# A gated recurrence's 128 by 128 score matmuls become pairs of 64-column tiles

## The chip, the cores and the metric

The kernel runs on one core of one Trainium2 chip. The metric is the device time of one execution in microseconds, the median of three runs. In the traces PE is TensorE (its matmuls; PEld are its weight loads), DVE is VectorE, ACT is ScalarE, POOL is GpSimd and SP is SyncE.

## The reference, cut to what matters

An encoder trunk of two layers is applied to two sequences, of 512 and of 256 tokens, with shared weights in fp32. Each layer is half a SwiGLU feed-forward, a token mixer, and another half feed-forward. Layer 0 mixes with a bidirectional gated linear recurrence (HGRN2), layer 1 with windowed attention. The recurrence is the part that is changed:

```python
def gla_chunk_scan(q, k, v, logf):
    """S_t = diag(f_t) S_{t-1} + k_t v_t^T, o_t = S_t^T q_t."""
    ...
o_fwd = gla_chunk_scan(q, k_f, i, logf_f)
rev = lambda a: jnp.flip(a, axis=1)
o_bwd = rev(gla_chunk_scan(rev(q), rev(k_b), rev(i), rev(logf_b)))
o = (o_fwd + o_bwd).astype(F32)
```

There are eight heads with keys and values of 128. Within 128 tokens the result is a 128 by 128 matrix A of scores (a query against each key, times all forget gates between the two) applied to the values; between such blocks a state is carried.

## The kernel before, in words

All 768 tokens of both sequences lie side by side, in six blocks of 128 (four and two). Feed-forward and projections split each fp32 factor into two parts of the faster fp32r type and sum three products (`mm3`, lines 254 to 256).

For each head `hgrn_proj` computes queries, keys and gates, transposed, with the 128 key channels on partitions. Then `hgrn_scan` builds A without ever dividing by a product of gates, over seven levels. At level l tokens form groups of 2^l, and level l fills the entries of A whose query and key lie in neighbouring groups of one pair. Level 6 thus fills the two 64 by 64 corners off the diagonal of a block, and levels 0 to 5 lie inside the two 64 by 64 corners on it. One more product, of the plain queries and the summed keys, fills the diagonal itself.

A level runs so:

1. ACT copies the level's keys together into `kop` (line 689), one buffer that all levels use.
2. PE multiplies, for each of the six blocks, `kop` by the level's queries (`scan_scores`, line 664): 128 by 128 by 128, in plain fp32. In the trace one such matmul is two weight loads and two MATMUL records. The blocks of the first sequence go to one PSUM bank, those of the second to another (`ps` tiles, eight banks in turn).
3. DVE merges the result into A (`put`): a copy at level 0 (line 678), and a copy under a mask of the level's entries elsewhere (line 683), one for each sequence.
4. DVE multiplies the queries by the gates (line 706), the keys by theirs (line 710) and the gates among themselves (line 712) for the next level. The queries may be changed only when PE has read them.

After the levels, the blocks' states and outputs follow (lines 726 to 765). `weave` issues the next head's projection in pieces between the levels of this one; the order on each engine is then set by the tile framework's scheduler, which the program leaves to it, and each engine runs its own instructions strictly in that order. Weights are staged ahead by ACT (line 166) and DVE (line 167).

Of the kernel before, what the change touches and what calls it, by code (L numbers as in the profile page):

```python
# [16 lines left out]
P = 128  # L17
# [5 lines left out]
T = TA + TB  # L23
NBLK = T // P
EPS = 1e-6
HEADS = 8
LEVELS = 7
# [6 lines left out]
SEQS = ((0, TA), (TA, TB))  # L34
# [13 lines left out]
class Trunk:  # L48
# [608 lines left out]
    def halves(self, t, l, par, d):  # L657
        return t[:, d, :].rearrange("p (b g j) -> p b g j", g=2, j=1 << l)[:, :, par, :]

    def scan_scores(self, pss, lhs, rhs):  # L660
        nc = self.nc
        for b in range(NBLK):
            s, i = (0, b) if b < 4 else (1, b - 4)
            nc.tensor.matmul(pss[s][:, i * P : (i + 1) * P], lhs(b), rhs(b), start=True, stop=True)  # L664

    def hgrn_scan(self, hd, v):
        nc = self.nc
        h, qs, kd, f, q, k = (hd[n] for n in ("h", "qs", "kd", "f", "q", "k"))
        ka = self.big([P, 2, T])
        kop, A = ka[:, 0, :], ka[:, 1, :]  # L670
        totals = self.big([P, 2, T])
        blk = lambda t, b: t[:, b * P : (b + 1) * P]

        def put(level, pss):
            for s, (off, n) in enumerate(SEQS):
                dst = A[:, off : off + n]
                if level == 0:
                    nc.vector.tensor_copy(dst, pss[s])
                    continue
                nb = n // P  # L680
                m = self.masks[:, level, :].unsqueeze(1).to_broadcast([P, nb, P])
                r = lambda t: t.rearrange("p (b j) -> p b j", b=nb)
                nc.vector.copy_predicated(r(dst), m, r(pss[s]))

        tot, base = f, 0
        for l in range(LEVELS):
            c, J = T >> l, 1 << l
            kv = bass.AP(k.tensor, k.offset, [list(k.ap[0]), [2 * J, c // 2], [T + J, 2], [1, J]])
            nc.scalar.copy(kop.rearrange("p (b g j) -> p b g j", g=2, j=J), kv)

            def rhs(b):
                return bass.AP(
                    q.tensor, q.offset + b * P, [list(q.ap[0]), [2 * J, P // (2 * J)], [T + J, 2], [1, J]]
                )

            pss = [self.ps(n) for _, n in SEQS]
            self.scan_scores(pss, lambda b: blk(kop, b), rhs)
            put(l, pss)
            if l == 0:
                pss = [self.ps(n) for _, n in SEQS]  # L700
                self.scan_scores(pss, lambda b: blk(kd, b), lambda b: blk(qs, b))
                put(LEVELS, pss)
            part = [list(q.ap[0])]
            both = bass.AP(q.tensor, q.offset, part + [[T + J, 2], [2 * J, c // 2], [1, J]])
            t = bass.AP(tot.tensor, tot.offset + base + 1, [list(tot.ap[0]), [T - 1, 2], [2, c // 2], [0, J]])
            nc.vector.tensor_mul(both, both, t)
            for d in range(2):
                xv = self.halves(k, l, d, d)
                t = tot[:, 1 - d, base + 1 - d : base + c : 2].unsqueeze(2).to_broadcast([P, c // 2, J])
                nc.vector.tensor_mul(xv, xv, t)  # L710
            nbase = 0 if l == 0 else base + c
            nc.vector.tensor_mul(
                totals[:, :, nbase : nbase + c // 2], tot[:, :, base : base + c : 2], tot[:, :, base + 1 : base + c : 2]
            )
            tot, base = totals, nbase
            yield

        F, Bk = 1, 0
        order = ((0, 0), (0, 1), (0, 2), (0, 4), (1, 1), (1, 2), (1, 3), (1, 5))
        kT = self.big([P, 8, P])  # L720
        S = self.big([P, 8, P])
        for half in range(2):
            pt = self.ps()
            for i in range(4):
                d, b = order[half * 4 + i]
                nc.tensor.transpose(pt[:, i * P : (i + 1) * P], blk(k[:, d, :], b), self.ident)
            nc.scalar.copy(kT[:, half * 4 : half * 4 + 4, :], pt.rearrange("p (a b) -> p a b", a=4))
        vb = lambda b: v[b][:, h * P : (h + 1) * P]
        pds = []
        for half in range(2):  # L730
            pd = self.ps()
            for i in range(4):
                d, b = order[half * 4 + i]
                nc.tensor.matmul(pd[:, i * P : (i + 1) * P], kT[:, half * 4 + i, :], vb(b), start=True, stop=True)
            pds.append(pd)
        state = {}
        for d, steps in ((0, ((0, None), (1, 0), (2, 1), (4, None))), (1, ((3, None), (2, 3), (1, 2), (5, None)))):
            for b, prev in steps:
                i = order.index((d, b))
                ds = pds[d][:, (i % 4) * P : (i % 4 + 1) * P]  # L740
                if prev is None:
                    nc.scalar.copy(S[:, i, :], ds)
                else:
                    dec = totals[:, 1 - d, base + b : base + b + 1]
                    nc.vector.scalar_tensor_tensor(S[:, i, :], S[:, order.index((d, prev)), :], dec, ds, ALU.mult, ALU.add)
                state[(d, b)] = S[:, i, :]
        yield
        pos = [self.ps(n) for _, n in SEQS]
        for b in range(NBLK):
            s, i = (0, b) if b < 4 else (1, b - 4)  # L750
            o = pos[s][:, i * P : (i + 1) * P]
            terms = [(blk(A, b), vb(b))]
            if (0, b - 1) in state and b != 4:
                terms.append((blk(q[:, F, :], b), state[(0, b - 1)]))
            if (1, b + 1) in state and b != 3:
                terms.append((blk(q[:, Bk, :], b), state[(1, b + 1)]))
            for j, (l_, r_) in enumerate(terms):
                nc.tensor.matmul(o, l_, r_, start=(j == 0), stop=(j == len(terms) - 1))  # L758
        for s, (off, n) in enumerate(SEQS):
            nb = n // P  # L760
            sq = self.tmp(n)
            nc.scalar.square(sq, pos[s])
            for b in range(nb):
                nc.scalar.copy(vb(off // P + b), pos[s][:, b * P : (b + 1) * P])
            nc.vector.tensor_reduce(
                self.hss[:, h, off // P : off // P + nb], sq.rearrange("p (b j) -> p b j", b=nb), AX.X, ALU.add
            )
# [507 lines left out]
```

## Time and profile before

| | |
|---|---|
| runs | 2866.38, 2866.47, 2860.94 us; median 2866.38 |
| span of the profiled execution, from the first to the last instruction | 2863.4 us |
| the recurrence's scan, eight heads | about 585 to 960 us of the span |
| MATMUL records of line 664 | 768 (two for each of 384 matmuls) |
| merges of lines 678 and 683 | 16 and 112 |
| granted TensorE clock, mean | 0.997 |

The profiled execution is one of its own; its page gives its span and no time beside it. A group of instructions in the profile is named by its line, engine, operation and tile; "128x512" is partitions by elements. Matmuls are pipelined, so a record's duration is longer than the distance from its start to the next one's. The chain of waits counts that distance, and the durations of records overlap.

### The profile page before, as it was taken

Reading aid. Unit: us, or ns where it says so; the run is one execution under the profiler, and the core shown is the slowest. Engines: PE = TensorE matmul, PEld = TensorE weight load, DVE = VectorE, ACT = ScalarE, POOL = GpSimd, SP = SyncE. Lnnn points to the kernel's source line nnn. Section 1 sums busy time; section 2 is a strip of 40 time slices with the busy share of each in tenths; the row PEclk is TensorE's granted clock in tenths of the full one; section 3 lists DMA queues with packets and bytes.
Section 4 is the critical chain, followed back from the end, with each engine's and each line's share of the span. In section 5 each row is a group of like instructions: output and inputs, shape, how many; then the busy total and the mean of one; then the engine's idle time right before and its main releaser. Section 6 shows DMA issues by size and latency. Waiting matters only on the chain.

```text
span 2863.4 us, 40520 instructions
## 1 busy us (share of the span) xinstructions
PE 2800.4 (98%) x15225; PEld 2556.8 (89%) x15225; DVE 2198.4 (77%) x3846; ACT 1318.5 (46%) x2454; POOL 304.4 (11%) x306
## 2 busy tenths in 40 slices
PE   8999999999999999999999999999999899999998
PEld 8899998889899889988998998999887779988997
DVE  7788788477577658788878877887859978778877
ACT  7344443434344435444445543444457755434443
POOL 1111120000000001111110111111000001111110
PEclk9999999999999999999999999999999999999999
DMA  6555454311111233555444355445412113554443
GB/s 166 126 124 125 116 133 119 109 45 38 52 38 30 74 88 89 133 129 124 118 118 109 88 134 126 121 119 122 126 63 74 45 38 92 132 129 120 120 122 96
DMA packets 330101, 291.37 MB, mean 102 GB/s; under 512 B 11608, under 2 KB 257840, under 8 KB 329904
## 3 DMA queue, kind: packets, MB, share of 16 engines
q1 hardware_dynamic: 294064, 212.43, 25.2%
q0 software_dynamic: 31680, 62.93, 12.5%
q10 hardware_dynamic: 4160, 13.42, 1.3%
q8 instruction: 119, 1.95, 0.3%
q14 instruction: 78, 0.64, 0.1%
HBM read 216.39 MB, written 9.44 MB: 79 GB/s over the span
## 4 chain that ended last, share of the span: by engine, by line
PE 68%; DVE 21%; DMA 5%; issue 3%; ACT 3%; DVEq 0%; ACTq 0%; POOLq 0%; SPq 0%
PE ps L414 24%; PE ps L472 11%; PE ps L254 8%; PE ps L255 8%; PE ps L256 8%; DVE w L200 5%; DVE big L260 3%; PE ps L664 3%; DVE x L494 3%; DMA wr<-wr 3%; DMA wr<-in_ffn_w_dram 3%; DVE tA L347 1%; DVE wr L206 1%; PE ps L758 1%; PE ps L316 1%
## 5 line engine op out<-in xcount | busy, mean ns | idle before, releaser
L414 PE MATMUL ps<-big,w 128*128 128x384 f32 x6720 | 1174.0, 335 | 6.6 <-DVE tA L437 6.2
L414 PEld LDWEIGHTS ps<-big,w 128*128 128x128 f32 x6720 | 1166.0, 188 | 12.7 <-DVE tA L437 11.2
L199 ACT CAST w<-wr 128x512 fp32r<-128x512 f32 x600 | 415.9, 707 | 724.2 <-PE ps L414 317.0
L472 PE MATMUL ps<-w,big 128*128 128x512 f32 x2520 | 587.2, 392 | 17.3 <-DVE x L494 17.3
L472 PEld LDWEIGHTS ps<-w,big 128*128 128x128 f32 x2520 | 470.4, 188 | 129.2 <-DVE x L494 16.6
L200 DVE TENSOR_TENSOR w<-wr,w 128x512 fp32r<-128x512 f32 (+1 forms) x520 | 437.1, 851 | 95.8 <-ACT w L199 87.1
L494 DVE SCALAR_TENSOR_TENSOR x<-ps,x 128x512 f32<-128x512 f32 x468 | 305.9, 683 | 20.4 <-PE ps L472 10.2
L141 POOL DMA_DIRECT2D s<-wr x120 | 105.6, 880 | 1619.8 <-DMA wr<-in_ffn_w_dram 585.7
L254 PE MATMUL ps<-w,big 128*128 128x512 f32 x624 | 248.9, 399 | 0.2
L256 PE MATMUL ps<-w,big 128*128 128x512 f32 x624 | 244.9, 393 | 2.2 <-DVE big L323 1.3
L255 PE MATMUL ps<-w,big 128*128 128x512 f32 x624 | 244.2, 391 | 0.0
L259 ACT CAST big<-tA 128x384 fp32r<-128x384 f32 x296 | 147.9, 513 | 178.9 <-DVE tA L442 77.1
L254 PE MATMUL ps<-big,w 128*128 128x384 f32 (+2 forms) x640 | 220.8, 346 | 3.4 <-ACT big L259 2.0
L255 PE MATMUL ps<-big,w 128*128 128x384 f32 (+2 forms) x640 | 216.9, 339 | 0.7 <-DVE big L260 0.5
L256 PE MATMUL ps<-big,w 128*128 128x384 f32 (+2 forms) x640 | 215.7, 337 | 0.0
L167 DVE TENSOR_TENSOR w<-wr,w 128x1024 fp32r<-128x1024 f32 x92 | 111.4, 1221 | 81.0 <-ACT w L166 56.9
L260 DVE TENSOR_TENSOR big<-tA,big 128x384 fp32r<-128x384 f32 x296 | 167.4, 576 | 8.1 <-ACT big L259 4.9
L205 DVE TENSOR_TENSOR wr<-wr,wr 128x512 f32<-128x512 f32 (+1 forms) x100 | 79.4, 794 | 119.1 <-DMA wr<-wr 89.7
L141 POOL DMA_DIRECT2D wr<-wr x100 | 87.2, 872 | 687.6 <-DVE tA L343 321.4
L166 ACT CAST w<-wr 128x1024 fp32r<-128x1024 f32 x92 | 96.6, 1052 | 120.3 <-PE ps L255 99.4
L256 PEld LDWEIGHTS ps<-w,big 128*128 128x128 f32 x624 | 117.1, 188 | 28.2 <-DVE big L323 2.0
L254 PEld LDWEIGHTS ps<-w,big 128*128 128x128 f32 x624 | 117.4, 188 | 22.4 <-issue 0.6
(170 smaller groups left out, 3296.8 us busy)
## 6 DMA issues: line engine op xcount, KB each, us to landing
wr<-in_ffn_w_dram SPq DMA_DIRECT2D x264, 512.0 KB, 3.9
s<-in_ffn_w_dram SPq DMA_DIRECT2D x120, 256.0 KB, 3.0
s<-wr POOLq DMA_DIRECT2D x120, 256.0 KB, 4.0
wr<-wr POOLq DMA_DIRECT2D x80, 256.0 KB, 3.8
wr<-in_hg_w_in_dram SPq DMA_DIRECT2D x40, 512.0 KB, 3.7
wr<-wr POOLq DMA_DIRECT2D x20, 512.0 KB, 4.6
spill<-x ACTq DMA_DIRECT2D x12, 512.0 KB, 3.1
x<-spill ACTq DMA_DIRECT2D x12, 512.0 KB, 3.3
```

Source lines behind the costliest of these rows:

```text
L141: self.nc.gpsimd.dma_start(out, src, accum_op=ALU.add)
L167: self.nc.vector.tensor_sub(lo, raw, hi.bitcast(F32))
L199: nc.scalar.copy(h, src)
L200: (eng or nc.vector).tensor_sub(l, src, h.bitcast(F32))
L254: nc.tensor.matmul(out, a[0], b[0], start=first, stop=False)
L255: nc.tensor.matmul(out, a[0], b[1], start=False, stop=False)
L256: nc.tensor.matmul(out, a[1], b[0], start=False, stop=last)
L259: self.nc.scalar.copy(hi, src)
L260: self.nc.vector.tensor_sub(lo, src, hi.bitcast(F32))
L414: self.nc.tensor.matmul(ps, a[x], b[y], start=first and k == 0 and i == 0, stop=k == 3 and i == 2, skip_group_check=True,)
L472: nc.tensor.matmul(ps, a[x], w[y], start=name == chain and kp == 0 and q == 0, stop=kp == 1 and q == 2, skip_group_check=True,)
L494: self.nc.vector.scalar_tensor_tensor(x, ps, c, x, ALU.mult, ALU.add)
```

## The change

Each 128 by 128 score matmul becomes two, for the two halves of a block's keys (`par`). Each has 64 columns of `kop` as weights, and streams only the 64 queries that those keys can meet: at levels 0 to 5 and for the diagonal those of the same half, at level 6 those of the other half. The first half writes partitions 0 to 63 of the bank, the second 64 to 127; in the instructions they are tiles of 128 rows by 64 columns of the array, at column 0 and at column 64. The corners that a level doesn't need are not computed any more. A level's scores are then 384 columns for both sequences, in one bank. The merge goes by partition halves, each over all six blocks; level 6 becomes a plain copy, since its corners are needed whole.

```diff
-    def scan_scores(self, pss, lhs, rhs):
-        nc = self.nc
+    def scan_scores(self, lhs, rhs):
+        ps = self.ps(NBLK * 64)
         for b in range(NBLK):
-            s, i = (0, b) if b < 4 else (1, b - 4)
-            nc.tensor.matmul(pss[s][:, i * P : (i + 1) * P], lhs(b), rhs(b), start=True, stop=True)
+            for par in range(2):
+                rows = slice(par * 64, (par + 1) * 64)
+                self.nc.tensor.matmul(ps[rows, b * 64 : (b + 1) * 64], lhs(b)[:, rows], rhs(b, par), start=True, stop=True)
+        return ps
...
-        def put(level, pss):
-            for s, (off, n) in enumerate(SEQS):
-                dst = A[:, off : off + n]
-                if level == 0:
-                    nc.vector.tensor_copy(dst, pss[s])
+        def put(level, ps):
+            for par in range(2):
+                rows = slice(par * 64, (par + 1) * 64)
+                c = 1 - par if level == LEVELS - 1 else par
+                dst = A.rearrange("p (b c j) -> p b c j", c=2, j=64)[rows, :, c, :]
+                src = ps[rows, :].rearrange("p (b j) -> p b j", j=64)
+                if level in (0, LEVELS - 1):
+                    nc.vector.tensor_copy(dst, src)
                     continue
-                nb = n // P
-                m = self.masks[:, level, :].unsqueeze(1).to_broadcast([P, nb, P])
-                r = lambda t: t.rearrange("p (b j) -> p b j", b=nb)
-                nc.vector.copy_predicated(r(dst), m, r(pss[s]))
+                m = self.masks[rows, level, c * 64 : (c + 1) * 64].unsqueeze(1).to_broadcast([64, NBLK, 64])
+                nc.vector.copy_predicated(dst, m, src)
...
-            pss = [self.ps(n) for _, n in SEQS]
-            self.scan_scores(pss, lambda b: blk(kop, b), rhs)
-            put(l, pss)
+            put(l, self.scan_scores(lambda b: blk(kop, b), rhs))
```

The scheduler's order changes with it on DVE. Its order at level 0 of the first head before (ps_5154 and ps_5155 are the banks of level 0, ps_5164 and ps_5165 those of the diagonal, big_5151 holds A, big_4938 the queries, big_4939 the keys, big_5152 the gates):

```order
L678 COPY big_5151<-ps_5154 128x512
L678 COPY big_5151<-ps_5155 128x256
L706 TENSOR_TENSOR big_4938<-big_4938,big_4937 128x2x384
L683 COPY_PREDICATED big_5151<-big_4691,ps_5164 128x512
L683 COPY_PREDICATED big_5151<-big_4691,ps_5165 128x256
L710 TENSOR_TENSOR big_4939<-big_4939,big_5152 128x192x2 x2
```

and after, where ps_5154 and ps_5169 are the two banks, and lines 708 and 712 are 706 and 710 of before:

```order
L683 COPY big_5151<-ps_5154 64x6x64 x2
L686 COPY_PREDICATED big_5151<-big_4691,ps_5169 64x6x64 x2
L708 TENSOR_TENSOR big_4938<-big_4938,big_4937 128x2x384
L712 TENSOR_TENSOR big_4939<-big_4939,big_5152 128x192x2 x2
```

The queries are now scaled behind the merge of the diagonal, where they were scaled ahead of it. On the other levels merge, queries and keys keep their order, except that in the fifth of the seven levels the keys are scaled in two parts, with a weight split between them.

More of the change, by code (lines that the diff above doesn't have):

```diff
@@ L689, in hgrn_scan, with rhs @@
             nc.scalar.copy(kop.rearrange("p (b g j) -> p b g j", g=2, j=J), kv)
[L691 to L694, printed above, removed]
-            pss = [self.ps(n) for _, n in SEQS]
-            self.scan_scores(pss, lambda b: blk(kop, b), rhs)
-            put(l, pss)
+            def rhs(b, par):
+                part = list(q.ap[0])
+                if J == 64:
+                    return bass.AP(q.tensor, q.offset + b * P + (0 if par else T + J), [part, [1, J]])
+                at = q.offset + b * P + par * 64
+                return bass.AP(q.tensor, at, [part, [2 * J, 64 // (2 * J)], [T + J, 2], [1, J]])
+            put(l, self.scan_scores(lambda b: blk(kop, b), rhs))
             if l == 0:
-                pss = [self.ps(n) for _, n in SEQS]
-                self.scan_scores(pss, lambda b: blk(kd, b), lambda b: blk(qs, b))
-                put(LEVELS, pss)
+                own = lambda b, par: qs[:, b * P + par * 64 : b * P + (par + 1) * 64]
+                put(LEVELS, self.scan_scores(lambda b: blk(kd, b), own))
             part = [list(q.ap[0])]
```

## The prediction

> **What bounds the kernel now.** I read the page first, then the stretches of the recurrence by engine, then the waits there, then the chain of waits through one head.
>
> ```profile
> span 2863.4 us, 40520 instructions
> ...
> PE 2800.4 (98%) x15225; PEld 2556.8 (89%) x15225; DVE 2198.4 (77%) x3846; ACT 1318.5 (46%) x2454; POOL 304.4 (11%) x306
> ```
>
> Busy shares over the whole span do not say what a change in one stage is worth, so the next view cuts out two of the eight heads of the scan. The columns are PE, PEld, DVE, ACT and POOL busy, then the granted clock and the DMA share.
>
> ```profile
> 628.70:671.40 42.70, 42.70 (x295) 39.38 (x294) 33.60 (x59) 17.50 (x34) 0.00 (x0) 1.00 0.13 38
> ...
> 714.00:789.40 75.40, 75.35 (x438) 66.35 (x437) 38.98 (x63) 25.03 (x44) 0.00 (x0) 1.00 0.18 50
> ```
>
> In an ordinary head PE fills all 42.70 us. DVE is busy for 33.60 us of them, 79%, and DMA is light. The clock is full. The next rows are from the waits of that stage (585 to 965 us): who waited for whom, total, times, longest.
>
> ```profile
> PE ps L664 <- ACT big L689: 1.7, 1, 1.7
> ...
> ACT big L689 <- PE ps L664: 63.6, 31, 6.0
> DVE big L683 <- PE ps L664: 41.1, 35, 6.2
> ```
>
> PE waits for others 1.7 us in 380; ACT and DVE wait for the score matmuls (L664) for 63.6 and 41.1 us. So PE time in this stage passes to the end of the program one for one, in both directions, and the question is what one level's scores cost PE. The chain through one head (start, length) gives that:
>
> ```profile
> 671.38 3.33 PE ps L664 x24
> ...
> 678.97 1.45 PE ps L664 x12
> ...
> 683.16 1.34 PE ps L664 x12
> ...
> 687.30 1.34 PE ps L664 x12
> ...
> 691.46 1.34 PE ps L664 x12
> ...
> 696.90 1.34 PE ps L664 x12
> ...
> 701.11 1.34 PE ps L664 x12
> ```
>
> Each fp32 matmul is two records, so 12 records are the six blocks of one level. A level costs 1.34 us, 112 ns a record (I call one a pass). The first group of 24 is level 0 and the tokens' own scores; with 1.34 for the latter, level 0 costs 1.99, 166 ns a pass. A head costs 3.33 + 1.45 + 5 x 1.34 = 11.48 us, eight heads 92 us. That is all the change works on.
>
> **The change, part by part.** *PE work.* Per level 12 passes of 128 columns by 128 become 24 passes of 64 by 64, in the order first half twice, second half twice, block after block. A 64-column pass streams for half of 112, 56 ns. Twice as many passes of half the length is no gain by itself: run one behind another they take what they took. The gain has to come from the two tiles, which use different columns of the array and different partitions of the bank, running at the same time. No row of this trace shows two matmuls at once, so I bound it.
>
> How fast passes can follow each other at that length is shown by the nearest row, the transposes in the attention stage (L903), which stream 128 columns in one go, and so about as briefly. From the chain there:
>
> ```profile
> 2103.64 0.23 PE ps L256
> 2103.86 0.63 PE ps L903 x8
> 2104.50 0.30 PE ps L254
> ```
>
> Eight in 0.63 us are 79 ns each, with a weight load of 128 columns before each. I take 79 ns as the pace of one tile, and 56 ns as its lower bound. With both tiles at work, a block needs two paces and not four, plus one pace at the group's end where the last tile has no partner.
>
> - At 79 ns: 6 x 158 + 79 = 1.03 us per group. Gain: six ordinary groups a head 6 x 0.31 = 1.88; level 1 0.42; level 0, whose strided passes take half of 166, 83 ns, 6 x 166 + 83 = 1.08, so 0.91. Together 3.21 us a head, **25.7 us** in eight.
> - At 56 ns: 0.73 us per group, 5.29 us a head, **42 us**. This is the other end of the gain.
> - Not at once: 24 x 79 = 1.90 us, a loss of 0.56 in the six, 0.45 and nothing (24 x 83 = 1.99), 3.81 a head, **30.5 us lost**; at 56 ns nothing gained or lost.
>
> I take the 79 ns with both tiles at work. The Trainium skill, TensorEngine Tiling (Array Packing), section Tiling Modes, says that different tiles can load weights and multiply in parallel; no run here shows it yet. Its page TensorE: Matmul & The Clock Gate, section LDWEIGHTS, prices a weight load at its columns over 1.2, about 107 ns for 128 and 53 for 64. By that a pass of 64 columns would be held by its 56 ns of streaming, and the sum would be the -28 us of the last rival below; the 79 ns above, which hold a load of 128 columns, disagree, and the trace decides.
>
> *The change of tile.* PE's order around one level in the middle of the scan (level 2 of head 0; ps_5245 and ps_5246 are the two banks of the two sequences, w the weights of the next head's projection), before:
>
> ```order
> L256 MATMUL ps_5210<-big_4595,w_4992 128x512
> L664 MATMUL ps_5245<-big_4938,big_5151 128x128 x4
> L664 MATMUL ps_5246<-big_4938,big_5151 128x128 x2
> L254 MATMUL ps_5210<-big_4596,w_4991 128x512
> L255 MATMUL ps_5210<-big_4596,w_4991 128x512
> ```
>
> and after:
>
> ```order
> L256 MATMUL ps_5220<-big_4595,w_4992 128x512
> L665 MATMUL ps_5260<-big_4938,big_5151 64x64 x12
> L254 MATMUL ps_5220<-big_4596,w_4991 128x512
> L255 MATMUL ps_5220<-big_4596,w_4991 128x512
> ```
>
> Nothing moved, but each group now stands between matmuls that use the whole array: 8 x 8 groups less the eight in which two follow each other directly leave 56 stretches, and 112 changes between whole and half arrays. Before there is none, so I bound one. Nothing at the low end. At the high end PE empties first:
>
> ```profile
> L664 PE MATMUL ps<-big 128*128 128x128 f32 x96 | 12.1, 275 | 0.0
> ```
>
> A pass whose successor starts after 112 ns lasts 275, so 163 ns of it are in flight; with the 79 - 56 = 23 ns of a load that nothing covers, 0.19 us. The nearest row is the L254 behind the transposes, quoted above: 0.30, which is 0.07 above the usual 0.23. A change of tile is more than a change of kind, so I take 0.13, midway: 112 x 0.13 = **14.6 us lost** (ends 0 and 21).
>
> *DVE.* Merges go from a sequence each (512 and 256 elements) to a partition half each (384 twice).
>
> ```profile
> L683 DVE COPY_PREDICATED big<-big,ps 128x512 f32<-128x512 uint8 x56 | 41.4, 740 | 41.2 <-PE ps L664 41.1
> ...
> L683 DVE COPY_PREDICATED big<-big,ps 128x256 f32<-128x256 uint8 x56 | 24.6, 439 | 0.0
> ```
>
> Time goes with elements along a partition: 384 come to 590 ns, two to 1.18 us as before (ends 0.88 and 1.48). That level 6 becomes a plain copy is worth hundredths. Both merges now wait for a group's last block, where the first used to start after two thirds. The timeline shows what covers that (PE's two groups, and DVE between them):
>
> ```profile
> 640.33 1.50 PE L664 MATMUL ps<-big,big 128*128 128x128 f32 x12
> ...
> 644.48 1.28 PE L664 MATMUL ps<-big,big 128*128 128x128 f32 x10
> ```
>
> ```profile
> 641.42 1.06 DVE L683 COPY_PREDICATED big<-big,ps 128x512 f32<-128x512 uint8 x2 [0.48 <-PE ps L664]
> 642.38 0.94 DVE L706 TENSOR_TENSOR big<-big,big 128x768 f32<-128x768 f32 x1
> ```
>
> The scaling of q (L706), which the next level's scores need, ends at 643.32, 1.16 us ahead of them. At level 0 it also moves behind the merge of the own scores, 1.18 us later; 30 projection matmuls, over 3 us, follow there. Both cost nothing while that lasts; gone, it would be a PE wait of some tenths per level. One bank per level instead of two: PE never waits for a bank here, so nothing.
>
> *Sum.* -25.7 + 14.6 = -11 us. A head shrinks from 42.7 to 41.3 us, where DVE's 33.6 are 81%, so it follows. The profiled span is 2863.4; the median of the runs, 2866.4, is 3.0 above it. So 2852 in the span, **2855 us** as measured. What a measurement can tell here is about 0.2%, 5.7 us.
>
> **Rivals.** *One behind another (slower).* The tiles do not overlap, since each pass needs its own weight load ahead and PE takes them in order; the place is each L665 group, the price 30.5 + 14.6 = 45 us: 2911. For it speaks that all 15,225 matmuls of this trace come one after another and that 79 ns are above the 56 streamed; against it only that halves of the array share nothing. It decides from 45 ns a pass: 24 x 45 = 1.08, which with two changes at 0.13 is the 1.34 of now.
>
> *Emptying eats the gain (no change).* PE runs empty at every change: 112 x 0.19 = 21 us against 25.7, -4 us: 2862. For it: 163 ns are in flight whenever a group begins or ends. Against: the 0.07 at L903. The Trainium skill, TensorEngine Tiling (Array Packing), section Tiling Modes, states that changing the tiling mode drains TensorE, without a time; no run here shows it yet.
>
> *Full overlap (faster still).* Tiles keep 56 ns: -42 + 14.6 = -28 us: 2839. DVE would then be at 33.6 of 39.3, 85%, and could still follow.
>
> **How the numbers follow.** Forecast (-11, own range 2845 to 2864) 0.40; one behind another 0.30; emptying 0.18; full overlap 0.12. Faster by over 0.2%: 0.29 of the forecast, 0.12 of full overlap, 0.04 of emptying, 0.45. Within 0.2%: 0.09, 0.09 and nothing else, 0.18. Slower: 0.02, 0.05 and 0.30, 0.37. The range runs from full overlap with changes at 0.07 (-42 + 8, 2832) to one behind another with a full emptying (+52, 2918), cut a little there, to 2914.
>
> **What would show it.** Right: a group of 24 passes (48 with the own scores) takes about 1.0 us in the chain, the L254 after it about 0.13 more than 0.23 in a few places, DVE merges 0.59 us, PE still full. One behind another: 1.9 us a group. Emptying: a hole of 0.2 us at both ends of each group. Wrong in a way I have not priced: DVE merges of 64 partitions above 0.74 us, or PE waiting for the scaling of q (L708 in the changed file) or for the copy of the keys (L692 there).

## The result and the profile after

| | before | after |
|---|---|---|
| median of the runs | 2866.28 us (4 runs) | 2845.23 us (4 runs) |
| span of the profiled execution | 2863.4 us | 2842.4 us |
| ratio | | 0.9935, 95% interval 0.9922 to 0.9948 |

The change made the kernel faster by 21 us, 0.65%. The forecast was 2855 us, the range 2832 to 2914. The page of after, the waits of PE in the scan, and one head between the same two points of its work as before (PE, PEld, DVE, ACT and POOL busy, granted clock, DMA):

```profile
span 2842.4 us, 42038 instructions
...
PE 2776.8 (98%) x15993; PEld 2516.0 (89%) x15993; DVE 2213.4 (78%) x3846; ACT 1317.8 (46%) x2454; POOL 303.5 (11%) x306
```

```profile
PE ps L665 <- ACT big L692: 3.4, 3, 1.7
PE ps L665 <- ACT big L647: 0.7, 1, 0.7
PE ps L665 <- DVE big L708: 0.2, 1, 0.2
```

```profile
626.80:666.40 39.60, 39.59 (x391) 34.27 (x390) 35.29 (x59) 17.33 (x34) 0.00 (x0) 1.00 0.14 41
```

There are 768 more matmul records and 23.6 us less PE time. A head takes 39.60 us where it took 42.70, and PE still fills it. DVE went from 33.60 to 35.29 us, 89%. The chain through a head (start, length):

```profile
666.42 1.85 PE ps L665 x48
668.27 0.32 PE ps L254
...
672.72 0.90 PE ps L665 x24
673.62 0.43 PE ps L254
...
676.56 0.85 PE ps L665 x24
677.41 0.43 PE ps L254
...
680.42 0.85 PE ps L665 x24
681.27 0.32 PE ps L254
```

A group takes 0.85 us in the chain, and the projection matmul behind it 0.20 more than usual (0.43 for 0.23, 0.32 for 0.12): 1.05 us a group, where it was 1.34. Level 1 takes 1.10 (1.45 before), and level 0 with the own scores 2.05 (3.33). A head saves 3.1 us on this, eight 25 us. Two rows of the timeline show what is inside a group, the first from a window of 0.04 us at its start:

```profile
636.88 0.28 PE L665 MATMUL ps<-big,big 128*64 128x64 f32 x2
```

```profile
636.88 0.92 PE L665 MATMUL ps<-big,big 128*64 128x64 f32 x24
```

Two passes of 0.27 us end within 0.28 us: they started within 10 ns of each other. And 24 passes are over in 0.92 us, of which the last record's 0.22 are its tail: 0.70 / 12 is 58 ns a pair. So the two tiles do work at the same time, each at about half of a full pass's 112 ns.

The sum of what the records show over the 56 stretches: passes cost 91.8 us before and 47.6 after, a gain of 44; 112 changes of tile cost 56 x 0.35 = 19.6 us, 0.17 each (with passes at 58 ns a pair, 1.05 - 0.70 is left for two); PE waits 2.6 us more (4.3 for 1.7), most of it in the seventh head and for ACT, which copies the keys (L692) and finishes a projection (L647). That is 22 us less, and the mixer as a whole, from the last up-product before it to the first behind it, shrank from 570.4 to 548.4 us. The rest of the program takes 1 us more.

DVE's merges, forecast at 0.59 us each, take 1.20 us for a level's two:

```profile
638.02 1.20 DVE L686 COPY_PREDICATED big<-big,ps 64x384 f32<-64x384 uint8 x2
639.24 0.96 DVE L708 TENSOR_TENSOR big<-big,big 128x768 f32<-128x768 f32 x1
```

### The profile page after: what moved, and what is told of

The parts are those of the page before. It is cut to its first block, busy times and chain, and to the rows that moved or that the text cites. A ratio compares the mean times of both kernels' runs of the same rounds, so it can differ in the third digit from the quotient of the medians.

```text
span 2842.4 us, 42038 instructions
## 1 busy us (share of the span) xinstructions
PE 2776.8 (98%) x15993; PEld 2516.0 (89%) x15993; DVE 2213.4 (78%) x3846; ACT 1317.8 (46%) x2454; POOL 303.5 (11%) x306
## 3 DMA queue, kind: packets, MB, share of 16 engines
q8 instruction: 125, 2.05, 0.3%
## 4 chain that ended last, share of the span: by engine, by line
PE 65%; DVE 23%; DMA 5%; issue 4%; ACT 3%; DVEq 0%; ACTq 0%; POOLq 0%; SPq 0%
PE ps L414 24%; PE ps L472 11%; PE ps L254 8%; PE ps L255 8%; PE ps L256 8%; DVE w L200 6%; DVE big L260 4%; DVE x L494 3%; DMA wr<-wr 2%; DMA wr<-in_ffn_w_dram 2%; PE ps L665 2%; DVE tA L347 1%; DVE wr L206 1%; PE ps L760 1%; DVE tA L448 1%
## 5 line engine op out<-in xcount | busy, mean ns | idle before, releaser
L414 PEld LDWEIGHTS ps<-big,w 128*128 128x128 f32 x6720 | 1167.0, 188 | 14.5 <-DVE tA L437 12.9
```

The source lines that it names most:

```text
L414: self.nc.tensor.matmul(ps, a[x], b[y], start=first and k == 0 and i == 0, stop=k == 3 and i == 2, skip_group_check=True,)
```

## The experiments

Each was timed against the kernel before on its own chip, so ratios are compared and not times. The code outside the mixer is the same in all of them, yet in the traces its time ranges from 2277 to 2295 us. Where that matters, the mixer's own time in the trace stands beside the ratio.

**One tile for both halves.** Both halves' matmuls go to columns 0 to 63 of the array, the second half's into a second bank; the merge moves it to the upper partitions.

```diff
-        ps = self.ps(NBLK * 64)
+        ps = [self.ps(NBLK * 64) for _ in range(2)]
...
-                self.nc.tensor.matmul(ps[rows, b * 64 : (b + 1) * 64], lhs(b)[:, rows], rhs(b, par), start=True, stop=True)
+                self.nc.tensor.matmul(ps[par][:64, b * 64 : (b + 1) * 64], lhs(b)[:, rows], rhs(b, par), start=True, stop=True)
...
-                src = ps[rows, :].rearrange("p (b j) -> p b j", j=64)
+                src = ps[par][:64, :].rearrange("p (b j) -> p b j", j=64)
...
```

> Both halves of a block go to the same tile of the array (columns 0 to 63, partitions 0 to 63 of two banks); as many matmuls of the same sizes, as many changes between whole and half array as in the changed kernel. Theory: the gain is two tiles streaming at once, 58 ns a pair. Then 24 passes here take 24 x 58 = 1.40 us a group where pairs take 0.70, level 0 24 x 84 = 2.0 instead of 1.0; 7 x 0.7 + 1.0 = 5.9 us a head, +47 us on 2845: 2892, slower than before. If the one tile also has to wait for its weight loads (79 ns a pass), 2915 to 2920. Rival: the gain is that the unneeded corners are not streamed any more and needs no second tile; then 2845, within 5 us.

Ratio 1.0087 (1.0069 to 1.0106): 25 us slower than before, 44 slower than after, where the theory had 47. A group on the timeline:

```profile
644.01 1.61 PE L665 MATMUL ps<-big,big 128*64 128x64 f32 x24
```

(1.61 - 0.22) / 24 is 58 ns a pass, one behind another. The same matmuls of the same sizes with the same changes of tile lose what the change gains: the gain is the overlap alone. Not streaming the unneeded corners saves nothing by itself. And the pace on one tile is 58 and not 79 ns, about half of a full pass's 112. A full pass loads 128 columns and streams 128 queries, one of these 64 and 64, so the run does not tell which of the two sets the 58.

**The halves in turn.** The loops over blocks and halves are exchanged.

```diff
-        for b in range(NBLK):
-            for par in range(2):
+        for par in range(2):
+            for b in range(NBLK):
```

> The changed kernel with the two loops of scan_scores exchanged: all six blocks of the first half, then all six of the second. Same tiles, same work, same result. Theory with PE taking matmuls strictly in order: nothing to overlap except at the middle of a group, so like one tile: +45 us, about 2890. Theory with PE reaching ahead for the other tile's matmuls (the first two passes of a group already start 6 ns apart in the trace, although each matmul has two passes on its own tile): if it reaches 12 passes ahead 2845, if it reaches only two or so 2890. Rival (fewer columns, no overlap needed): 2845.

Ratio 1.0033 (1.0022 to 1.0045): 28 us slower than after, between both expectations. Three windows that begin 0.02 us ahead of one group, 0.52, 0.56 and 0.73 us long, show why (count of passes at the end of each row), and the whole group:

```profile
639.92 0.68 PE L665 MATMUL ps<-big,big 128*64 128x64 f32 x8
```

```profile
639.92 0.79 PE L665 MATMUL ps<-big,big 128*64 128x64 f32 x10
```

```profile
639.92 0.91 PE L665 MATMUL ps<-big,big 128*64 128x64 f32 x15
```

```profile
639.92 1.43 PE L665 MATMUL ps<-big,big 128*64 128x64 f32 x24
```

Eight passes start one by one, then the 9th and another together, then more in pairs. One tile is paced at 58 ns, so the second of two passes that start together is the other tile's first, the 13th in the program, ahead of the 10th, 11th and 12th. The single records bear this out. In nearly all groups of 24 a tile's first pass lasts 270 ns and the others 222: with one tile only the first pass of a group lasts 270, in the changed kernel the first two, and here the first and the tenth to start. PE thus starts a matmul ahead of three that wait for their tile, and not further ahead. Both my expectations were too simple: it reaches ahead, but not over half a group. In the changed kernel, where tiles alternate every two passes, that reach is enough, and it is why pairs form though both passes of a matmul go to the same tile. The Trainium skill, TensorE: Matmul & The Clock Gate, section The mechanism, says that matmuls start and end strictly in program order; by the counts in the rows above this run disagrees on the start: the 13th pass goes ahead of the 10th.

**One more full-array matmul in every group, after and before.** The identity by itself into unused columns of a bank, behind the third block: with two changes of tile in the changed kernel, with none in the kernel before.

```diff
-        ps = self.ps(NBLK * 64)
+        ps_all = self.ps(512)
+        ps = ps_all[:, : NBLK * 64]
         for b in range(NBLK):
+            if b == 3:
+                self.nc.tensor.matmul(ps_all[:, 384:512], self.identr, self.identr, start=True, stop=True)
             for par in range(2):
```

> The changed kernel, with one more matmul over the whole array (the identity by itself, 128 by 128, into unused columns of the level's bank) in the middle of every group of scores: 64 of them, each a pass of 56 to 79 ns, and 128 more changes between half and whole array. Theory: each change costs 0.17 us whenever it happens, so 64 x (0.34 + 0.08) = +27 us, 2872. Rival: the 0.34 us at the ends of a stretch belong to something else (weights not loaded ahead after a wait for ACT, or the semaphores there), then only the passes count: +4 to +5 us, 2850.

> The control for the run before: the kernel before with the same extra matmul in the middle of every group (in unused columns of the second sequence's bank). No change of tile here. Both theories: 64 passes of 56 to 79 ns, +4 to +5 us on 2866: 2871.

After: 1.0012 (1.0002 to 1.0021), 22 us over the changed kernel's 0.9935. Before: 1.0036 (1.0023 to 1.0049), 10 us, where 4 to 5 were expected. A group after, and one before:

```profile
640.08 0.57 PE L668 MATMUL ps<-big,big 128*64 128x64 f32 x12
640.58 0.33 PE L665 MATMUL ps<-ident_r 128*128 128x128 f32 x1
640.84 0.57 PE L668 MATMUL ps<-big,big 128*64 128x64 f32 x12
```

```profile
642.40 0.83 PE L666 MATMUL ps<-big,big 128*128 128x128 f32 x6
642.99 0.31 PE L665 MATMUL ps<-ident_r 128*128 128x128 f32 x1
643.13 0.88 PE L666 MATMUL ps<-big,big 128*128 128x128 f32 x6
```

After, the second half of the group starts 0.76 us behind the first, where six pairs take 0.35: 0.41 more. Before, it starts 0.73 behind, where six passes take 0.67: 0.06, and 0.05 more behind it (0.88 for 0.83), 0.11. The two changes are the difference, 0.30 us, 0.15 each, close to the 0.17 at the ends of a stretch. The whole times say less: 22 and 10 us leave 12 for the 128 changes, 0.09 each, with about 0.1% of uncertainty in each ratio. The mixer alone is 24.1 us longer after (572.5) and 7.4 before (577.8), while PE's idle time in it fell from 5.0 to 2.8 us after and went from 2.3 to 2.5 before. Without these waits 19 us are left, 0.15 each, as in the rows. So a change of tile has its price wherever it stands, with nothing waited for. The Trainium skill, TensorEngine Tiling (Array Packing), section Tiling Modes, says that changing the mode drains TensorE: by the trace it costs 0.15 to 0.17 us here, about the 163 ns that the prediction read as in flight. That the array empties is not shown beyond this size.

**Thirty-two columns.** The changed kernel again as a base, the change carried on to four tiles of 32 columns at levels 0 to 4 and for the diagonal, the plain copies of levels 0 and 6 on ACT, and both.

```diff
-    def scan_scores(self, lhs, rhs):
-        ps = self.ps(NBLK * 64)
+    def scan_scores(self, lhs, rhs, w=64):
+        ps = self.ps(NBLK * w)
         for b in range(NBLK):
-            for par in range(2):
+            for par in range(P // w):
...
+            w = 32 if l < 5 else 64
```

```diff
                 if level in (0, LEVELS - 1):
-                    nc.vector.tensor_copy(dst, src)
+                    nc.scalar.copy(dst, src)
```

> The changed kernel once more, as the base of the three runs beside it on this chip: 0.9935 of the kernel before.

> At levels 0 to 4 and for the diagonal, whose entries lie in 32 by 32 corners, each score matmul becomes four tiles of 32 columns; levels 5 and 6 stay as in the changed kernel; the merges of the six groups go by quarters of the partitions (four of 192 elements, by the slope of the rows 0.36 us each, 1.46 a level instead of 1.19). If the four tiles run at once and a pass keeps halving (29 ns), a group takes 0.35 us less in five levels and 0.5 less at level 0 and 0.35 for the diagonal: about 2.1 us a head, 17 us in all, less what DVE, then busy for 35 of 37 us a head, cannot follow: 0.988 to 0.992 of before. If a pass doesn't get shorter than 58 ns (its weight load) or PE reaches only 4 passes ahead, as in the run with the halves in turn (its ninth pass of the first half starts with the first of the second), so that three of four tiles overlap at best: no gain or a loss of up to 10 us on the changed kernel, 0.993 to 0.997.

> The changed kernel, with the plain copies of levels 0 and 6 done by ACT, not by DVE: 4 x 0.56 = 2.2 us a head off DVE, about 2 us a head on ACT. Theory: in the stage PE is the bound and DVE covered, so only the new waits of PE in the last two heads (3 us together) can shrink: 0.9925 to 0.9945 of before. Rival: DVE sets the pace of the levels since the change; then up to 2.2 us a head come back, 17 us: 0.9875.

> Both together: the 32-column tiles and the plain copies on ACT. If the 32-column tiles gain on PE and DVE is what they run into, this is the fastest: 0.987 to 0.989 of before. If they gain nothing on PE, as the changed kernel, 0.993 to 0.996.

| | ratio | interval |
|---|---|---|
| changed kernel again | 0.9925 | 0.9912 to 0.9937 |
| 32 columns | 0.9910 | 0.9895 to 0.9925 |
| copies on ACT | 0.9912 | 0.9899 to 0.9926 |
| both | 0.9894 | 0.9880 to 0.9909 |

Copies on ACT alone, just below the range expected, can't be told from the changed kernel, though DVE lost 2 us a head. The mixer takes 548.8 us, where it took 548.3 in the changed kernel beside it: DVE did not set its pace. With 32 columns the groups shrank as the first expectation had it, and waits took back more than that: the mixer takes 555.2 us, 548.6 with the copies on ACT as well, and PE is idle in it for 24.1 and 18.0 us, not 5.1. The lower ratios of these two runs, of which only that of both is clear of the noise, thus come from outside the mixer. That they lie in the expected ranges or next to them is luck, and I have no cause for it. A group on the timeline of the run with the tiles alone, PE's waits in its scan, and its merges:

```profile
637.84 0.62 PE L665 MATMUL ps<-big,big 128*32 128x32 f32 x48 [0.65 <-DVE big L712]
```

```profile
PE ps L665 <- DVE big L712: 13.3, 25, 1.1
PE ps L665 <- ACT big L695: 8.4, 8, 2.4
```

```profile
L689 DVE COPY_PREDICATED big<-big,ps 32x192 f32<-32x192 uint8 x160 | 59.4, 371 | 10.0 <-PE ps L665 6.5
```

48 passes are over in 0.62 us, 0.43 without the last one's tail. At the 29 ns a pass of the changed kernel's 64 columns, halved for 32, two tiles would take 48 x 14.5 = 0.70 us, so more than two run at once. But a level's merge is now four of 371 ns, 1.48 us, and from level 2 on PE waits before most groups: for the scaled queries (L712 in that file) 13.3 us in 25 waits, for the keys' copy 8.4 in 8.

**A compact merge.** Levels are merged into an array in which all corners of a block have the same columns, so one merge takes all partitions. ACT spreads it into A once a head, and does the copies of the levels that fill whole corners.

```diff
+            if level == 0:
+                nc.vector.tensor_copy(C, ps)
+            elif level == LEVELS or 2 << level <= WC:
+                m = self.masks[:, level, :].unsqueeze(1).to_broadcast([P, NBLK, WC])
+                nc.vector.copy_predicated(vw(C, WC), m, vw(ps, WC))
...
+            if level == 5:
+                spread(C, WC)
```

> The changed kernel's 64-column tiles, but the levels are merged into a compact array of 128 partitions by 6 x 64, where both halves of a block have the same place, so that a merge is one of 384 elements and not two; ACT spreads it into A once a head (two copies) and copies level 6 there. DVE loses about 7 x 0.59 + 1.1 = 5.2 us a head, PE does what it did. Theory (PE bounds the stage, DVE covered): only the waits of PE that came with the change can shrink, 5 us at most: 0.9905 to 0.9925 of before. Rival (DVE sets the pace of the changed kernel): up to 5 us a head, 0.980 to 0.985.

> The 32-column tiles with the compact merge (128 partitions by 6 x 32, one merge of 192 elements, 0.36 us, at six of the eight groups); levels 5 and 6 and the spreading of the compact array (four copies a head) on ACT. In the run with 32-column tiles PE's groups took 0.64 us where the 64-column ones take 1.05, and 25.9 us went into PE waiting for DVE and ACT. Theory: the waits were DVE's; with DVE down by 7 us a head they go to under 5 us, and the whole gain of the tiles shows: 77.4 - 25.9 + 5 = 56 us in the groups against 72, so 16 us below the changed kernel, 0.985 to 0.988 of before. Rival: the waits are a chain through ACT (its copy of the keys) that stays, and more work on ACT lengthens it: 0.989 to 0.992.

With 64 columns 0.9916 (0.9903 to 0.9929), as the theory of a covered DVE has it: with DVE down by 5 us a head only waits shrink. The mixer takes 546.6 us, 1.8 less than in the changed kernel, and PE is idle in it for 2.3 us and not 5.0. With 32 columns **0.9839 (0.9826 to 0.9853)**, median 2814.42 us against 2860.96: faster than both kernels. The merge, PE's waits in the scan, and a group:

```profile
L696 DVE COPY_PREDICATED tA<-big,ps 128x192 f32<-128x192 uint8 x40 | 15.0, 374 | 17.8 <-PE ps L668 17.7
```

```profile
PE ps L668 <- ACT big L708: 2.5, 7, 0.4
```

```profile
638.02 0.63 PE L668 MATMUL ps<-big,big 128*32 128x32 f32 x48
```

One merge of 374 ns does what four of 371 did, and DVE now waits for PE (17.7 us), not PE for DVE. The mixer takes 532.3 us (548.4 in the changed kernel), 16 less, as forecast. The remaining 10 us of the gain over the changed kernel lie outside the mixer, most of them in the feed-forward layers, whose code is the same; PE is idle there for 41 us in this trace and for 42 to 53 in the others, and I have no cause for that. This part is open.

## Why the prediction was right or wrong

- *PE bounds the scan, and its time passes to the end one for one*: right. The groups and the waits lost 22 us, the program 21. Taking half of DVE's merges away (compact, 64 columns) or its copies alone changed nothing measurable in the whole time.
- *Two tiles at once*: right. One tile for both costs all of it, 44 us.
- *Their pace, 79 ns from the transposes*: wrong, and the term is mis-sized: the passes gave 44 us, not 25.7. It is 58 ns, close to the other end of that bound. The eight transposes load 128 columns for each 128 streamed in one go; here the load has 64. The smaller load may be why; it was not tried alone.
- *The change of tile, 0.13 us*: too low, 0.17, so 19.6 us and not 14.6; the bound of 0.19, from the passes in flight, was nearer than the row of another kind of switch. The rival of emptying was thus nearly right about the price and wrong about the sum, since the gain was larger too. The two errors leaned against each other, 18 us too little gained and 5 too little lost, which brought the forecast nearer than its terms were: -11 forecast, -21 measured.
- *DVE covered*: right, with less to spare. A merge was read as 2 x 0.59 = 1.18 "as before". On the chip, one by one, they are that, but before, two overlapped to 1.06 us (the row in the prediction), and now they take 1.20 to 1.22. The scaling of the queries, too, started 0.10 us ahead of the merges' end (642.38 against 642.48) and now starts behind it (639.24 against 639.22). DVE is busy for 35.29 us a head where I had 33.6.
- *No new waits*: wrong by 2.6 us, most of it in the seventh head, where PE waits for ACT.
- *One behind another*: wrong, and its price was too high: 45 us forecast, 25 measured with both halves on one tile; the 79 ns again are the difference. Its rule, that the change loses from 45 ns a pass (41 with the measured changes, (1.34 - 0.35) / 24), fits the runs: 29 ns a pass on average is a gain, 58 a loss.
- *Full overlap*: this rival had the pace that was measured, and the -21 lies a little nearer to its -28 than to the -11. The dearer changes and the new waits are what it lacked.

## What to carry to other kernels

Two half-width matmuls gain only if they use different columns of the array and stand close together in the program: alternate the tiles, since in the run with the halves in turn PE reached ahead over three waiting passes and no further. Count the changes between whole and split array at 0.15 to 0.17 us each, and gather the split matmuls into stretches; a stretch must save over 0.35 us. And plan the merge with the tiles: by partition quarters PE lost more in waits for it than the tiles saved (mixer 555.2 us, 548.4 with 64 columns), while in a layout where all partitions share their columns the mixer fell to 532.3. The kernel gained 1.6% over the first one in all, a part of it outside the mixer and unexplained.

## What the runs showed of the hardware that was not expected

- A matmul can start ahead of three earlier ones that wait for their tile (13th pass with the 9th).
- A pass of 32 columns on four tiles still shrinks: 48 in 0.43 us, 36 ns for each four, where 24 of 64 columns on two tiles took 0.70, 58 ns for each two.
- Two merges of 128 partitions back to back took 1.06 us for 512 and 256 elements, 0.12 less than their durations together (740 and 439 ns). Two of 64 partitions and 384 elements took 1.20 to 1.22 and did not overlap (594 ns each). The PSUM bank is not why: in the run with one tile for both halves the two read two banks, and all 48 pairs took 1.17 to 1.21 us with a gap between them. Whether it is the 64 partitions was not tried alone.
